# Recurrent states of a streaming encoder: two at a time inside the last feed-forward

## The chip, the cores and the metric

The kernel runs on one core of a Trainium2 chip. The metric is device time in microseconds (us), read as the median of several runs. A core has five engines with a queue of their own each: TensorE (PE in the profile, its weight loads PEld), VectorE (DVE), ScalarE (ACT), GpSimd (POOL), and SyncE (SP), which here only issues DMAs. An engine takes its instructions in the order in which they stand in its queue.

## The reference

Two layers of an encoder work on 512 frames of a new stream and on 8 running streams of 16 frames each, 640 rows of 1024 channels. Each layer is a feed-forward, a mixer, and another feed-forward, each followed by a LayerNorm of `ALPHA * x + sublayer(x)`. The feed-forward is

```
def swiglu(x, w_gate, w_up, w_down):
    return (jax.nn.silu(x @ w_gate) * (x @ w_up)) @ w_down
```

with 2816 hidden channels. The mixer of the second layer carries a recurrent state of 32 heads x 64 x 128 for each running stream, and the new state is an output:

```
h_new = h * jnp.exp(cs[:, -1])[..., None, None] + jnp.einsum('bsgr,bsgn,bsgrp->bgrpn', to_end, b_c, x_c)
```

It is a scaling of the old state by one number for each head, plus a product over the 16 new frames. All is in fp32.

## The kernel before

The kernel does six phases in turn: `ffn0`, `mix0`, `ffn1`, `ffn2`, `mix1`, `ffn3`. Every fp32 operand of a product is split into a high part (a cast on ScalarE, L100) and the rest (a subtraction on VectorE, L101), and three products of the parts stand for one. Weights come as tiles of 128 x 1024 through four `raw` places (L119, L340, L341, L468 issue the loads, all on SP).

**The feed-forward** (`ffn`, L226) takes 22 tiles of 128 hidden channels. Two go ahead; then five groups of four follow. In a group, `pair` (L399) does two tiles at a time: the gate products, and the up products, with a scheme of seven products of blocks for eight (`matrix`, L369, 84 matmuls at L365 for one call). Between the gate and the up products of a group's first pair stands the down projection of the group before (`down`, L535). In `ffn1`, `ffn2` and `ffn3` a down projection of four tiles is `down7` (L462), again seven products (L501), each for two row tiles, ahead of which the row tile of the running streams is done with 24 plain matmuls (L146). The seven products share six PSUM banks. Of each product, one row tile is added to `yacc` by VectorE (L510). The other is scaled by ScalarE into one of three `ev` buffers (L513), and a DMA that accumulates, issued by GpSimd, adds it to `yacc` (L514). The first and the second of these accumulations go to the same part of `yacc`. The first and the last down projections of a feed-forward are done with plain matmuls.

**The states.** The new states of the running streams are not made in the mixer. It leaves the rows that are needed in memory (`xb`), and the decays (`el`). `ssd_states` (L1457) makes the states inside `ffn3`: it is a generator, and `tick` (L235) advances it by one step at certain places: behind each gate and each up product pair, behind some row tiles of the first and the last down projection, and in `down7` behind its second and its fifth product (L530). That makes seven calls in the first group of four tiles (gate, three in the down projection, up, gate, up), six in each of the other four (gate, two in the down projection, up, gate, up), and three in the last down projection.

There are 32 states (4 groups of heads x 8 streams) of 128 x 512. For two streams at a time, twelve row loads (L1473 into `xrow`, L1474 into `brow`) bring three copies of 16 rows for each. Then, for each of the two: a load of the old state (L1478) into one of two places `h0`; and in the next step the product (L1481, one matmul into a bank of `pst`), the scaling by the decay on GpSimd (L1483), the addition of the product on VectorE (L1484), and the store (L1485). All loads and stores are issued by SP. In the profile `h0` is written `h`, and `pst` is written `bank`.

A scheduler lays out each engine's queue ahead of time. It goes by the order in which the instructions are written and by when it expects their inputs: an instruction whose inputs are ready can be placed ahead of one that was written before it. A tile with several places makes a new user wait until the last reader of the place is done.

Of the kernel before, what the change touches and what calls it, by code (L numbers as in the profile page):

```python
# [9 lines left out]
F32 = mybir.dt.float32  # L10
# [3 lines left out]
ALU = mybir.AluOpType  # L14
# [22 lines left out]
def kernel(ctx: ExitStack, tc: tile.TileContext, I, O, phases=PHASES):  # L37
    nc = tc.nc
# [1418 lines left out]
    def ssd_states(wk):  # L1457

        el8 = wk.tile([128, 4, 8, 8], F32, name="el8")
        nc.sync.dma_start(el8.rearrange("p g b h -> p g (b h)"), ssd["el"])  # L1460


        xrow = wk.tile([128, 512], F32R, name="xrow", bufs=1)
        brow = wk.tile([128, 2, 128], F32R, name="brow", bufs=1)
        nc.vector.memset(xrow.bitcast(F32), 0.0)
        nc.vector.memset(brow.bitcast(F32), 0.0)
        for g, b2, q in ((g, b2, q) for g in range(4) for b2 in range(2) for q in range(2)):
            for h in range(2):
                for r, (sx, sb) in enumerate(((0, 0), (0, 1), (1, 0))):
                    rows = slice(64 * h + 16 * r, 64 * h + 16 * r + 16)  # L1470
                    t0 = 64 * h + 32 * b2 + 16 * q
                    src = lambda s, a, b: ssd["xb"][g][s, t0:t0 + 16, a:b]
                    nc.sync.dma_start(xrow[rows].bitcast(F32), src(sx, 0, 512))  # L1473
                    nc.sync.dma_start(brow[rows, h].bitcast(F32), src(sb, 512, 640))  # L1474
            for h in range(2):
                n = 4 * h + 2 * b2 + q
                h0 = wk.tile([128, 512], F32, name="h0", bufs=2)
                nc.sync.dma_start(h0, I["ssd_h0"][g, n])  # L1478
                yield
                pst = state["pst"]()  # L1480
                nc.tensor.matmul(pst, brow[:, h], xrow, start=True, stop=True)  # L1481
                h4 = h0.rearrange("p (h d) -> p h d", d=64)
                nc.gpsimd.tensor_tensor(h4, h4, el8[:, g, n, :, None].to_broadcast([128, 8, 64]), op=ALU.mult)  # L1483
                nc.vector.tensor_tensor(h0, h0, pst, op=ALU.add)  # L1484
                nc.sync.dma_start(O["ssd_s"][g, n], h0)  # L1485

    def mixer1(ph, last):
        V, G = nc.vector, nc.gpsimd
# [391 lines left out]
    for ph in phases:  # L1880
        last = ph == phases[-1]
        if ph.startswith("ffn"):
            ffn(int(ph[3]), ph, last, sides.get(ph))
        elif ph == "mix0":
            mixer0(ph, last)
        else:
            mixer1(ph, last)
            if "ffn3" not in phases:
                with ExitStack() as st:
                    for _ in ssd_states(pool("ssd", 1, st, reuse_waits="tile")):  # L1890
                        pass
# [112 lines left out]
```

## Time and profile before

| | us |
|---|---|
| median of 3 runs | 2552.12 |
| lowest, highest | 2546.31, 2556.58 |
| profiled execution | 2550.71 |
| its span, first to last instruction | 2549.0 |
| weight load by SP in the whole profile, `w_gate`, to landing | 3.6 |
| accumulating DMA in the whole profile, to landing | 5.3 |

The side work lies between 2109 us, where the first row load is issued, and 2531 us, where the last state is stored. In rows of the timeline the columns are start and duration in us, engine, line, operation, output and input tiles, shape and count, and in brackets the idle time of the engine just before, with the instruction or DMA that ended it. Rows of waits give the waiting engine with its line, what it waited for, the total in us, the number of times, and the longest. A group of instructions by line is followed by its busy us, the mean of one in ns, and the idle time before it.

### The profile page before, as it was taken

What the parts mean: (1) busy time and instruction counts of PE and PEld (TensorE: products, weight loads), DVE (VectorE), ACT (ScalarE), POOL (GpSimd) and SP (SyncE); (2) the same over time, 40 slices, a digit from 0 to 9 for tenths busy, and PEclk for the clock granted to TensorE, in tenths of its full rate; (3) what the DMA queues carried; (4) which work ended last, traced back from release to release, by engine and by line L of the source; (5) the groups of instructions that cost most, each with busy time, mean ns of one, the idle gap of its engine ahead of it and who ended that gap; (6) DMA issues with size and microseconds to landing.
All of it is one profiled execution on the core that took longest, in us unless ns stands there. A gap on an engine that the chain in (4) does not pass through costs nothing. (4 is left out here: it accounts for less than half of the span.)

```text
span 2549.0 us, 40847 instructions
## 1 busy us (share of the span) xinstructions
PE 2501.2 (98%) x15551; PEld 2289.7 (90%) x15551; DVE 2013.0 (79%) x3505; ACT 1273.8 (50%) x2389; POOL 374.5 (15%) x492
## 2 busy tenths in 40 slices
PE   9999999999999999999999999999999999999998
PEld 9999999878789999999999999988989889898887
DVE  7788777666879888878988887777576789898877
ACT  4443444436744555554555554566565543555542
POOL 0000001210130000013000002211121251111111
PEclk9999999999999999999999999999999999999999
DMA  5332335443222433361244443456464723445553
GB/s 185 108 106 87 105 112 154 147 165 110 73 83 63 117 102 108 105 170 50 67 120 112 112 119 103 136 182 196 142 212 140 242 66 107 146 146 155 162 161 123
DMA packets 179253, 324.80 MB, mean 127 GB/s; under 512 B 21312, under 2 KB 92608, under 8 KB 178544
## 3 DMA queue, kind: packets, MB, share of 16 engines
q1 hardware_dynamic: 165200, 293.83, 36.5%
q0 software_dynamic: 13856, 28.35, 5.8%
q8 instruction: 122, 2.00, 0.3%
q14 instruction: 75, 0.61, 0.1%
HBM read 259.56 MB, written 40.54 MB: 118 GB/s over the span
## 5 line engine op out<-in xcount | busy, mean ns | idle before, releaser
L101 DVE TENSOR_TENSOR w<-raw,w 128x512 fp32r<-128x512 f32 (+2 forms) x721 | 627.6, 892 | 94.9 <-ACT w L100 92.0
L100 ACT CAST w<-raw 128x512 fp32r<-128x512 f32 (+1 forms) x721 | 532.7, 769 | 324.7 <-DVE raw L348 153.0
L365 PE MATMUL bank<-xhi,w 128*128 128x320 f32 x2432 | 540.6, 309 | 2.1 <-DVE hf L417 1.3
L146 PE MATMUL bank<-xhi,w 128*128 128x256 f32 (+2 forms) x2272 | 498.1, 311 | 1.6 <-ACT xhi L210 1.0
L365 PE MATMUL bank<-T,w 128*128 128x320 f32 x2736 | 427.0, 309 | 2.8 <-ACT bank L382 2.3
L365 PEld LDWEIGHTS bank<-xhi,w 128*128 128x128 f32 x2432 | 407.4, 188 | 8.4 <-DVE hf L417 3.7
L365 PEld LDWEIGHTS bank<-T,w 128*128 128x128 f32 x2736 | 406.9, 188 | 4.2 <-ACT bank L382 2.8
L146 PEld LDWEIGHTS bank<-xhi,w 128*128 128x128 f32 x2272 | 377.7, 188 | 11.6 <-issue 5.2
L365 PE MATMUL bank<-xlo,w 128*128 128x320 f32 x1216 | 375.0, 308 | 0.0
L146 PE MATMUL bank<-xlo,w 128*128 128x256 f32 (+2 forms) x1136 | 351.2, 310 | 1.9 <-DVE xlo L211 1.7
L146 PE MATMUL bank<-w,h 128*128 128x512 f32 x1488 | 346.6, 391 | 0.0
L146 PEld LDWEIGHTS bank<-w,h 128*128 128x128 f32 x1488 | 277.4, 188 | 57.3 <-ACT h L100 1.4
L365 PEld LDWEIGHTS bank<-xlo,w 128*128 128x128 f32 x1216 | 228.0, 188 | 0.0
L146 PEld LDWEIGHTS bank<-xlo,w 128*128 128x128 f32 x1136 | 213.9, 188 | 4.9 <-DVE xlo L211 2.0
L348 DVE TENSOR_TENSOR raw<-raw 128x512 f32<-128x512 f32 x304 | 210.7, 693 | 3.2
L514 POOL DMA_DIRECT2D yacc<-ev x84 | 73.6, 943 | 693.7 <-ACT ev L513 600.2
L501 PE MATMUL bank<-w,h 128*128 128x512 f32 x576 | 139.2, 396 | 6.9 <-ACT ev L513 6.9
L501 PEld LDWEIGHTS bank<-w,h 128*128 128x128 f32 x576 | 109.8, 191 | 31.2 <-ACT ev L513 8.2
L378 ACT COPY mx<-bank 128x320 f32<-128x320 f32 x152 | 64.7, 426 | 110.1 <-PE bank L365 109.5
L510 DVE SCALAR_TENSOR_TENSOR yacc<-bank,yacc 128x512 f32<-128x512 f32 x84 | 57.8, 689 | 69.3 <-PE bank L501 69.2
L223 DVE SCALAR_TENSOR_TENSOR yacc<-bank,yacc 128x512 f32<-128x512 f32 x120 | 81.8, 686 | 34.4 <-PE bank L146 33.9
L513 ACT ACTIVATE ev<-bank 128x512 f32<-128x512 f32 x84 | 50.3, 599 | 115.4 <-PE bank L501 95.1
(431 smaller groups left out, 3440.4 us busy)
## 6 DMA issues: line engine op xcount, KB each, us to landing
raw<-in_w_gate_dram SPq DMA_DIRECT2D x88, 512.0 KB, 3.6
raw<-in_w_up_dram SPq DMA_DIRECT2D x88, 512.0 KB, 4.1
raw<-in_w_down_dram SPq DMA_DIRECT2D x88, 512.0 KB, 3.6
raw<-in_m_in_dram SPq DMA_DIRECT2D x52, 512.0 KB, 4.6
yacc<-ev POOLq DMA_DIRECT2D x84, 256.0 KB, 5.3
raw<-in_m_out_dram SPq DMA_DIRECT2D x24, 512.0 KB, 4.2
csb<-cs_d SPq DMA_DIRECT2D x20, 512.0 KB, 5.4
h<-in_ssd_h_dram SPq DMA_DIRECT2D x16, 512.0 KB, 6.2
```

What stands on the lines that cost most here:

```text
L100: nc.scalar.copy(hi, src)
L101: return nc.vector.tensor_tensor(lo, src, hi.bitcast(F32), op=ALU.subtract)
L146: state["pe"] = nc.tensor.matmul(ps, a, b, start=(k == 0), stop=(k == n - 1)).ins
L223: state["acc"] = nc.vector.scalar_tensor_tensor(ya, pb, scale, ya, op0=ALU.mult, op1=ALU.add).ins
L348: V.tensor_tensor(o, v, w, op=ALU.subtract)
L365: nc.tensor.matmul(ps, A[p][:, a, k * 128:k * 128 + 128], X[p][b][:, k, :], start=(first and n == 0), stop=(n == 11), skip_group_check=True)
L378: nc.scalar.copy(e[n], ps)
L501: nc.tensor.matmul(ps, a[:, u], b[:, v], start=(first and n == 0), stop=(n == 5), skip_group_check=True)
L510: V.scalar_tensor_tensor(ya, ps, 0.5 / ALPHA, ya, op0=ALU.mult, op1=ALU.add)
L513: nc.scalar.mul(e, ps, 0.5 / ALPHA)
L514: nc.gpsimd.dma_start(yacc[:, t, 512 * j:512 * j + 512], e, accum_op=ALU.add)
```

## The change

Both states of a pair are handled in one step of the generator, and moves and arithmetic are in different steps. One step issues the stores of the pair before, the twelve row loads and the two loads of old states. The next does, for each of the two, the scaling, the product and the addition. The last pair is stored behind the loop. `h0` has three places in place of two, so that 2 KB more are taken in each partition while `ffn3` runs. The scaling is now written ahead of the product. The number of steps stays at 32, with the end of the generator in the 33rd call.

```diff
+        done = []
         for g, b2, q in ((g, b2, q) for g in range(4) for b2 in range(2) for q in range(2)):
+            for o, h0 in done:
+                nc.sync.dma_start(o, h0)
             for h in range(2):
                 for r, (sx, sb) in enumerate(((0, 0), (0, 1), (1, 0))):
                     rows = slice(64 * h + 16 * r, 64 * h + 16 * r + 16)
...
                     nc.sync.dma_start(xrow[rows].bitcast(F32), src(sx, 0, 512))
                     nc.sync.dma_start(brow[rows, h].bitcast(F32), src(sb, 512, 640))
+            done = []
             for h in range(2):
                 n = 4 * h + 2 * b2 + q
-                h0 = wk.tile([128, 512], F32, name="h0", bufs=2)
-                nc.sync.dma_start(h0, I["ssd_h0"][g, n])
-                yield
+                done.append((O["ssd_s"][g, n], wk.tile([128, 512], F32, name="h0", bufs=3)))
+                nc.sync.dma_start(done[h][1], I["ssd_h0"][g, n])
+            yield
+            for h, (_, h0) in enumerate(done):
+                h4 = h0.rearrange("p (h d) -> p h d", d=64)
+                nc.gpsimd.tensor_tensor(h4, h4, el8[:, g, 4 * h + 2 * b2 + q, :, None].to_broadcast([128, 8, 64]),
+                                        op=ALU.mult)
                 pst = state["pst"]()
                 nc.tensor.matmul(pst, brow[:, h], xrow, start=True, stop=True)
-                h4 = h0.rearrange("p (h d) -> p h d", d=64)
-                nc.gpsimd.tensor_tensor(h4, h4, el8[:, g, n, :, None].to_broadcast([128, 8, 64]), op=ALU.mult)
                 nc.vector.tensor_tensor(h0, h0, pst, op=ALU.add)
-                nc.sync.dma_start(O["ssd_s"][g, n], h0)
+            yield
+        for o, h0 in done:
+            nc.sync.dma_start(o, h0)
```

## The prediction

> **What bounds the kernel now.** I read the page's busy shares first, then stretches of the timeline, then TensorE's waits, then the chain of waits around the longest of them.
>
> ```profile
> span 2549.0 us, 40847 instructions
> PE 2501.2 (98%) x15551; PEld 2289.7 (90%) x15551; DVE 2013.0 (79%) x3505; ACT 1273.8 (50%) x2389; POOL 374.5 (15%) x492
> ```
>
> The span is 2549.0 us and TensorE is busy for 2501.2 of it. The change touches only the last feed-forward, so I asked for the busy time of that stretch (up to TensorE's last product), and of 100 us of an earlier feed-forward with the same products and no side work. Columns: stretch, its length, busy us of PE, PEld, DVE, ACT, POOL, granted clock, DMA share, GB/s.
>
> ```profile
> 1420.00:1520.00 100.00, 100.00 (x575) 92.26 (x574) 80.11 (x119) 51.74 (x83) 9.49 (x11) 1.00 0.44 117
> ...
> 2107.00:2540.00 433.00, 422.45 (x2468) 391.21 (x2467) 371.72 (x578) 198.80 (x337) 71.89 (x67) 0.99 0.49 144
> ```
>
> TensorE idles 433.00 - 422.45 = 10.55 us here and none at all there. The change adds and removes no product, so these 10.55 us and whatever a lowered clock costs are all that it can win. TensorE's waits in the last feed-forward, longest first, are led by one group, and three rows of TensorE's timeline hold it:
>
> ```profile
> PE bank L501 <- ACT ev L513: 6.9, 3, 3.4
> ```
> ```profile
> 2311.65 4.61 PE L501 MATMUL bank<-w,h 128*128 128x512 f32 x12 [3.41 <-ACT ev L513]
> ...
> 2390.81 3.01 PE L501 MATMUL bank<-w,h 128*128 128x512 f32 x12 [1.72 <-ACT ev L513]
> ...
> 2468.52 4.59 PE L501 MATMUL bank<-w,h 128*128 128x512 f32 x12 [1.79 <-ACT ev L513]
> ```
>
> Each is the last product of one of the three later seven-product down projections (bracket: idle before it). They idle 3.41 + 1.72 + 1.79 = 6.92 us. The twelve matmuls behind them are slow too. The chain around the first shows what twelve cost undisturbed, and what they wait for:
>
> ```profile
> 2291.47 5.44 PE bank L501 x24
> ...
> 2303.26 0.48 POOL yacc L514
> ...
> 2303.78 7.12 DMA yacc<-ev
> ...
> 2311.00 0.61 ACT ev L513
> ...
> 2311.65 4.61 PE bank L501 x12
> ```
>
> 24 take 5.44, so 12 take 2.72; the three groups lose 1.89, 0.29 and 1.87, together 4.05 us. So the stall is worth 6.92 + 4.05 = 10.97 us. It waits for an eviction (L513), that for one of three `ev` buffers, and that for an accumulating DMA which GpSimd issues (L514). I followed GpSimd's queue back to the first accumulation of each projection, with the eviction that feeds it:
>
> ```profile
> 2292.86 0.60 ACT L513 ACTIVATE ev<-bank 128x512 f32<-128x512 f32 x1 [0.17 <-PE bank L501]
> ...
> 2373.71 0.60 ACT L513 ACTIVATE ev<-bank 128x512 f32<-128x512 f32 x1
> ...
> 2451.35 0.60 ACT L513 ACTIVATE ev<-bank 128x512 f32<-128x512 f32 x1 [0.17 <-PE bank L501]
> ```
> ```profile
> 2293.48 1.38 POOL L1483 TENSOR_TENSOR h<-h,el 128x512 f32<-128x512 f32 x1 [9.86 <-DMA h<-in_ssd_h_dram]
> 2294.80 0.89 POOL L514 DMA_DIRECT2D yacc<-ev  x1
> 2303.24 2.65 POOL L514 DMA_DIRECT2D yacc<-ev  x3 [7.55 <-ACT ev L513]
> ...
> 2375.71 0.89 POOL L514 DMA_DIRECT2D yacc<-ev  x1
> ...
> 2453.29 0.88 POOL L514 DMA_DIRECT2D yacc<-ev  x1
> ```
>
> The evictions end at 2293.46, 2374.31 and 2451.95; the accumulations go at 2294.80, 2375.71 and 2453.29, which is 1.34, 1.40 and 1.34 us later. The first row shows why: the scaling of a state (L1483) stands ahead of the accumulation in GpSimd's order and has waited for its load. The second accumulation adds to the same part of `yacc` as the first and so waits until that has landed; the third and fourth stand behind it. A late first one therefore shifts the whole chain. The load comes late because of SP's queue:
>
> ```profile
> 2286.90 0.41 SPq L1485 DMA_DIRECT2D out_ssd_s_dram<-h  x1
> 2287.36 0.43 SPq L1474 DMA_DIRECT2D brow<-xb_d  x1
> 2289.11 0.35 SPq L340 DMA_DIRECT2D raw<-in_w_up_dram  x1
> 2289.56 0.38 SPq L1478 DMA_DIRECT2D h<-in_ssd_h_dram  x1
> ```
>
> The store of the state before (needs VectorE's addition), then a weight load (needs a free `raw` place), and only then the load. The other half of the stall is how long accumulations take. From the DMA issues (count, KB, us to landing), first of the second feed-forward, then of the last:
>
> ```profile
> yacc<-ev POOLq DMA_DIRECT2D x21, 256.0 KB, 5.3
> ```
> ```profile
> h<-in_ssd_h_dram SPq DMA_DIRECT2D x32, 256.0 KB, 3.4
> out_ssd_s_dram<-h SPq DMA_DIRECT2D x32, 256.0 KB, 2.1
> yacc<-ev POOLq DMA_DIRECT2D x28, 256.0 KB, 6.3
> ```
>
> 5.3 us without the states' traffic, 6.3 with it.
>
> **The change part by part.** Work is conserved: 32 products, 32 scalings, 32 additions, 32 loads, 32 stores and 192 row loads before and after, in 33 steps. Counted over the calls of the side work (seven in the first group of four tiles, six in each later group), an even call now computes and an odd one stores and loads. So in each later group the call ahead of the down projection computes, the one behind its second product only moves data, and the one behind its fifth product computes.
>
> ```profile
> L1483 POOL TENSOR_TENSOR h<-h,el 128x512 f32<-128x512 f32 x32 | 42.9, 1342 | 275.3 <-DMA h<-in_ssd_h_dram 218.3 <-DVE raw L478 26.6 <-DVE s L407 20.0
> ...
> L1484 DVE TENSOR_TENSOR h<-h,bank 128x512 f32<-128x512 f32 x32 | 21.7, 680 | 4.8 <-PE bank L1481 4.4 <-issue 0.4
> ```
>
> *Scaling a step behind its load.* The states computed ahead of a down projection were loaded at least one step earlier, so their scalings are over before it, and the first accumulation can go as its eviction ends. That takes 1.34, 1.40 and 1.34 us out of the three stalls, which become 2.07, 0.32 and 0.45: gain 4.08 us. If GpSimd still holds the accumulation, the gain is nothing.
>
> *The lowered clock.* 1.79 us of idle cost 1.87 and 1.72 cost 0.29, so idle of 0.32 and 0.45 should cost nothing: gain up to 0.29 + 1.87 = 2.16. The first stall, at 2.07, lies above both, so I leave its 1.89. Rows of the granted clock after the second and third:
>
> ```profile
> 2391.00:2393.00 2.00, 2.00 (x10) 1.00 0.42 147
> ...
> 2470.00:2472.00 2.00, 2.00 (x6) 0.50 0.52 137
> ```
>
> The Trainium skill (TensorE: Matmul & The Clock Gate, Part 1: The HAM clock gate) says that the clock halves after an idle window of about 3.4 us. Here 1.79 us was enough for 0.50, so the measurement decides; by the page a stall of 2.07 us would keep the full clock and all 4.05 us would come back: 8.1 us ahead of the costs below, against 6.2.
>
> *SP's queue.* A step of moves is two stores, twelve row loads and two state loads, 16 issues. The pitch of such a run is 2276.09 - 2275.62 = 0.47 us:
>
> ```profile
> 2275.62 0.42 SPq L1474 DMA_DIRECT2D brow<-xb_d  x1
> 2276.09 0.42 SPq L1473 DMA_DIRECT2D xrow<-xb_d  x1
> ```
>
> That is 7.5 us in one run instead of two runs of about 2 and 14 issues. Weight loads behind it (L340, L341, L468) start up to 7.5 us later; today the second run already puts 6.6 us in front of some, and no weight load appears among TensorE's waits, so I cost it at nothing; if that cover were gone, the step's extra 0.9 us per pair would be paid, 14 us over 16 pairs. The store now waits for an addition of an earlier step, so it holds nobody. With three places, the second load waits for the first store of the pair before to land, 2.1 us, while the twelve row loads in between fill 5.6: hidden.
>
> *Additions in pairs.* A second addition waits 0.68 us for the first, and a VectorE instruction behind the pair waits 0.68 more than now. VectorE is busy for 372 of the 433 us, so I bound this between 0 and 0.68 x 3 = 2 us at the three projections and take 0.3.
>
> *Bytes beside the accumulations.* In each of those projections two pairs of stores and loads now come in bursts, at the call ahead of it and at the one behind its fifth product. The nearest rows are 5.3 and 6.3 us: at best the traffic leaves the accumulations alone (1 us for each of two in the chain, 6 us over three projections), at worst it costs as much again. The bytes are the same and I see no reason for either sign, but a burst is more likely to meet the first accumulation, so I take a loss of 0.3 us a projection, 0.9.
>
> Sum: 4.08 + 2.16 - 0.3 - 0.9 = 5.0 us. The profiled execution took 2550.7 us, 1.4 below the median of the three runs (2552.1), so I expect 2545.7 for such an execution and a median of **2547**.
>
> **The rivals.** *A, the forecast:* 2547.
>
> *B, the whole stall goes:* the first accumulation goes earlier and lands faster too. 10.97 us less than the median is 2541. For: no such stall where there is no side work. Against: it needs both halves at once.
>
> *C, nothing to measure:* the instructions do not keep to their steps. For: the `brow` load at 2287.36 belongs to the following call, and was issued as soon as the product had freed its rows; scalings, too, run as soon as their load lands. Then the second state of a pair is still loaded late, or the accumulations meet a thicker burst that eats the 5 us: 2552. The Trainium skill (DMA: Bandwidth & Descriptors, Issuing engines are not separate DMA queues) states a rule that speaks for this: transfers of all issuing engines run on the same 16 engines and interleave. The 6.3 against 5.3 us above agrees.
>
> *D, slower:* a pair's second scaling takes its place ahead of the first accumulation, as one does now, but its load stands behind two stores and twelve row loads. 14 x 0.47 = 6.6 us after the computing call, plus 3.4 to land and 1.34 to scale, is 11.3; today the accumulation goes 2294.80 - 2285.80 = 9.0 us after the call's product.
>
> ```profile
> 2285.80 0.23 PE bank L1481
> ```
>
> So the accumulation goes 2.3 us later, or 4.0 with a weight load's wait in front, as the one of 1.75 us between the issues at 2287.36 and 2289.11: I take 3.5 for each of three stalls, 2 for the first of the four projections, and the lowered clock in that one and in the second stall, 1.9 + 1.6: 10.5 + 2 + 3.5 = 16 us, 2568. It decides once that scaling precedes the accumulation and its load is issued later than 9.0 - 1.3 - 3.4 = 4.3 us after the product. Against: orders follow when a load is expected, and one behind 14 issues is expected late.
>
> **How the numbers follow.** A 0.45, B 0.15, C 0.25, D 0.15. Half a per cent, 12.8 us, is about what a measurement of this kernel can tell from no change. A, B and C all lie within it; B with a little luck beyond gives faster 0.05. D lies beyond it for most of its span: slower 0.12. Same 0.83. The range takes A, B but its end, C and the lower edge of D: 2539 to 2563.
>
> **What would show it.** Right: at the first accumulation of each down projection, GpSimd no longer comes out of a scaling, and it is issued within 0.2 us of its eviction; the three bracketed waits fall to about 2.1, 0.3 and 0.4; the stretch's idle falls from 10.55 to near 6. C shows as the same brackets with longer landings than 6.3; D as a scaling with a longer wait for its load right ahead of the first accumulation. Wrong altogether would be new waits for weights (L101, L365), or idle time of TensorE before L1481.

## The result and the profile after

| | before, us | changed, us |
|---|---|---|
| median of 7 runs each | 2549.5 | 2541.18 |
| lowest, highest | 2544.44, 2556.58 | 2537.88, 2543.43 |
| profiled execution | 2550.71 | 2543.04 |
| its span | 2549.0 | 2541.3 |

The changed kernel takes 0.9966 of the time before (95% interval 0.9952 to 0.998); the medians differ by 8.3 us. The forecast was a median of 2547; rival B, the whole stall gone, was 2541. The spans differ by 7.7 us. The page's head of the changed kernel:

```profile
span 2541.3 us, 40809 instructions
...
PE 2500.3 (98%) x15551; PEld 2289.3 (90%) x15551; DVE 2015.3 (79%) x3505; ACT 1272.5 (50%) x2389; POOL 376.2 (15%) x492
```

The same work is done; what went is time in which TensorE waited or ran slowly. Here is the last feed-forward up to TensorE's last product in busy time by stretches (us, then busy PE, PEld, DVE, ACT, POOL, granted clock, DMA share, GB/s), and below it TensorE's waits in it (total, times, longest).

```profile
2107.00:2533.00 426.00, 420.59 (x2472) 389.34 (x2470) 375.54 (x580) 197.74 (x337) 76.48 (x67) 1.00 0.50 146
```
```profile
PE bank L365 <- ACT bank L382: 1.6, 5, 0.4
PE bank L365 <- DVE s L407: 1.4, 3, 0.5
PE bank L365 <- DVE w L101: 0.7, 1, 0.7
PE bank L365 <- ACT mx L378: 0.7, 1, 0.7
PE bank L365 <- ACT w L100: 0.6, 1, 0.6
```

Idle time is 426.00 - 420.59 = 5.41 us, in place of 10.55. The wait of the products L501 for evictions, 6.9 us before, is not among the rows at all. But small waits of L365 have grown: these five rows give 5.0 us, where the kernel before has 2.6, in four rows:

```profile
PE bank L365 <- ACT bank L382: 1.0, 1, 1.0
PE bank L365 <- DVE hf L417: 0.9, 3, 0.4
PE bank L365 <- DVE w L101: 0.5, 1, 0.5
...
PE bank L365 <- DVE s L407: 0.2, 1, 0.2
```

The groups of TensorE's products in that stretch, by their shapes (busy us, mean ns, idle before), before and then changed:

```profile
L365 PE MATMUL bank<-T,w 128*128 128x320 f32 x684 | 107.4, 309 | 1.5 <-ACT bank L382 1.0 <-DVE w L101 0.5
...
L501 PE MATMUL bank<-w,h 128*128 128x512 f32 x192 | 49.5, 411 | 6.9 <-ACT ev L513 6.9
```
```profile
L365 PE MATMUL bank<-T,w 128*128 128x320 f32 x684 | 109.1, 310 | 3.0 <-ACT bank L382 1.6 <-DVE w L101 0.7 <-ACT w L100 0.6
...
L501 PE MATMUL bank<-w,h 128*128 128x512 f32 x192 | 44.8, 389 | 0.0
```

The same 192 matmuls take 49.5 - 44.8 = 4.7 us less. Most of that is the slow groups behind the stalls, which are gone with the stalls. Undisturbed, 24 such matmuls stand in one row:

```profile
2306.75 5.60 PE L501 MATMUL bank<-w,h 128*128 128x512 f32 x24
```

Twelve reach 2.72 us before the next one starts, so twelve take 5.60 - 2.72 = 2.88 us to the end of the last, and the rows of 4.61, 3.01 and 4.59 us before were 1.73, 0.13 and 1.71 too long, together 3.57. The stretch is 433 - 426 = 7.0 us shorter, of the 7.7 between the spans: 10.55 - 5.41 = 5.1 us are idle time, and 422.45 - 420.59 = 1.9 us are busy time. So half of what the slow matmuls gave was taken by other products: L365 has 1.7 us more. (Groups by line overlap at their ends, so their differences do not add up to the total.)

**The first accumulation.** ScalarE's eviction, GpSimd's queue, and SP's load of a state, around the second of the four seven-product down projections, then around the fourth, changed kernel:

```profile
2294.26 0.60 ACT L513 ACTIVATE ev<-bank 128x512 f32<-128x512 f32 x1 [2.88 <-PE bank L501]
...
2448.43 0.60 ACT L513 ACTIVATE ev<-bank 128x512 f32<-128x512 f32 x1 [2.88 <-PE bank L501]
```
```profile
2294.17 1.04 POOL L1486 TENSOR_TENSOR h<-h,el 128x512 f32<-128x512 f32 x1 [2.98 <-DVE yacc L522]
2295.15 0.88 POOL L514 DMA_DIRECT2D yacc<-ev  x1
2299.65 1.81 POOL L514 DMA_DIRECT2D yacc<-ev  x2 [3.61 <-DMA yacc<-ev]
...
2449.33 1.04 POOL L1486 TENSOR_TENSOR h<-h,el 128x512 f32<-128x512 f32 x1 [3.96 <-issue]
2450.31 0.87 POOL L514 DMA_DIRECT2D yacc<-ev  x1
```
```profile
2290.11 0.43 SPq L1482 DMA_DIRECT2D h<-in_ssd_h_dram  x1
```

A scaling (L1486, before L1483) still comes right ahead of the first accumulation, and it still waits for its load. The load goes at 2290.11, where it went at 2289.56 before, and lands 3.9 us later. The scaling starts 0.1 us after that, here and in the two later projections, whatever its bracket names. In the second projection the accumulation goes 2295.15 - 2294.86 = 0.29 us after the eviction's end, but in the fourth 2450.31 - 2449.03 = 1.28, nearly the 1.34 of before. What did change in every one is how long the accumulation then takes. The line of landing times of that one instruction, before and then changed:

```profile
DMA to landing us min/median/max: 7.7/7.7/7.7
```
```profile
DMA to landing us min/median/max: 3.8/3.8/3.8
```

For all 28 the median fell from 6.3 to 4.6 us.

SP's queue tells what the first accumulation met. Before, it was issued at 2294.80; the rows are SP's big loads near it:

```profile
2293.98 0.33 SPq L341 DMA_DIRECT2D raw<-in_w_up_dram  x1
2296.08 0.33 SPq L340 DMA_DIRECT2D raw<-in_w_gate_dram  x1
```

One 512 KB load went 0.8 us ahead and the next 1.3 us behind, with stores and rows from 2297 on. In the changed kernel it was issued at 2295.15:

```profile
2292.90 0.33 SPq L341 DMA_DIRECT2D raw<-in_w_up_dram  x1
2297.47 0.33 SPq L340 DMA_DIRECT2D raw<-in_w_gate_dram  x1
2298.60 0.33 SPq L341 DMA_DIRECT2D raw<-in_w_gate_dram  x1
2306.72 0.33 SPq L1477 DMA_DIRECT2D brow<-xb_d  x1
```

Here the nearest loads are 2.3 us away on either side, and no row or store of the states comes before 2306.72. The products of the pair (L1489) that the text of the change puts ahead of this down projection stand well before it:

```profile
2277.27 0.63 PE L1489 MATMUL bank<-xrow,brow 128*128 128x512 f32 x2
```

The scheduler drew them forward into the gate products, so the burst of stores, rows and loads behind them was out by 2290.5.

### The profile page after: what moved, and what is told of

Same layout as the page of the kernel before. It is cut to its first block, busy times and chain, and to the rows that moved or that the text cites. A ratio compares the mean times of both kernels' runs of the same rounds, so it can differ in the third digit from the quotient of the medians.

```text
span 2541.3 us, 40809 instructions
## 1 busy us (share of the span) xinstructions
PE 2500.3 (98%) x15551; PEld 2289.3 (90%) x15551; DVE 2015.3 (79%) x3505; ACT 1272.5 (50%) x2389; POOL 376.2 (15%) x492
## 5 line engine op out<-in xcount | busy, mean ns | idle before, releaser
L101 DVE TENSOR_TENSOR w<-raw,w 128x512 fp32r<-128x512 f32 (+2 forms) x721 | 625.0, 889 | 87.5 <-ACT w L100 84.7
L365 PE MATMUL bank<-xhi,w 128*128 128x320 f32 x2432 | 540.4, 309 | 2.9 <-DVE s L407 1.9
L365 PE MATMUL bank<-T,w 128*128 128x320 f32 x2736 | 428.7, 309 | 3.0 <-ACT bank L382 1.6
L365 PEld LDWEIGHTS bank<-xhi,w 128*128 128x128 f32 x2432 | 406.6, 188 | 8.8 <-DVE s L407 3.1
L365 PEld LDWEIGHTS bank<-T,w 128*128 128x128 f32 x2736 | 407.0, 188 | 6.3 <-ACT bank L382 4.2
L146 PEld LDWEIGHTS bank<-xhi,w 128*128 128x128 f32 x2272 | 380.0, 189 | 11.9 <-issue 5.1
L365 PE MATMUL bank<-xlo,w 128*128 128x320 f32 x1216 | 375.0, 308 | 0.0
L365 PEld LDWEIGHTS bank<-xlo,w 128*128 128x128 f32 x1216 | 228.0, 187 | 0.0
L501 PE MATMUL bank<-w,h 128*128 128x512 f32 x576 | 134.5, 389 | 0.0
L501 PEld LDWEIGHTS bank<-w,h 128*128 128x128 f32 x576 | 108.1, 188 | 22.5
```

The lines of the kernel that those rows point to most:

```text
L101: return nc.vector.tensor_tensor(lo, src, hi.bitcast(F32), op=ALU.subtract)
L146: state["pe"] = nc.tensor.matmul(ps, a, b, start=(k == 0), stop=(k == n - 1)).ins
L365: nc.tensor.matmul(ps, A[p][:, a, k * 128:k * 128 + 128], X[p][b][:, k, :], start=(first and n == 0), stop=(n == 11), skip_group_check=True)
L501: nc.tensor.matmul(ps, a[:, u], b[:, v], start=(first and n == 0), stop=(n == 5), skip_group_check=True)
```

## The experiments

All ratios are to the kernel before, run beside it, with 95% intervals. Two readings serve throughout: the *hold* of a first accumulation (its issue less the end of its eviction) and the *landings*. After the first runs they could be put into one sum. The products' evictions share three `ev` places, and the last product (fourth product of the scheme, into banks `x`) waits for the sixth accumulating eviction, which needs the place of the third accumulation. The third is issued right behind the second, and the second waits until the first has landed. So the chain is: hold + (first to third issue) + landing of the third, from the end of the first eviction. Each is read from the start and the landing of the single instructions. TensorE's own products set the deadline: undisturbed, the last product starts 14.6 us after the end of the first eviction (2309.47 - 2294.86 in the changed kernel), and the sixth eviction, 0.6 us, stands between the third landing and it, which leaves 14.0.

| kernel | chain in the four projections, us | TensorE's idle at L501 behind evictions, us |
|---|---|---|
| before | 10.8, 17.4, 15.7, 15.8 | 0, 3.41, 1.72, 1.79 |
| changed | 11.5, 11.2, 11.9, 11.1 | none |
| before, no scaling | 10.6, 11.9, 11.9, 11.6 | none |
| changed, one step later | 13.7, 14.1, 14.2, 13.3 | none |
| before, three places | 10.6, 11.5, 11.7, 11.8 | none |
| changed, two places | 15.7, 13.7, 14.9, 14.4 | 1.64, 0, 0.83, 0.34 |
| before, rows once | 13.2, 13.2, 12.6, 12.9 | none |
| changed, scaling on ScalarE | 12.0, 11.6, 11.6, 12.4 | none |
| changed, no scaling | 11.2, 11.1, 11.9, 11.6 | none |
| changed, held again | 12.5, 13.7, 13.4, 16.4 | 0, 0, 0, 2.37 |
| changed, twin stores | 12.4, 12.2, 13.7, 11.6 | none |
| changed, twin stores and hold | 12.6, 14.3, 13.7, 16.8 | 0, 0.27, 0, 2.41 |

All nine stalls have chains of 14.3 us or more. Eight equal the chain less 14.0; the ninth (16.8) equals the chain less 14.4, as TensorE itself came to its last product 0.3 us later there. The 39 chains of 14.2 or less show no such wait; the two above 14.0 among them, both of one step later, cost 0.2 us or less. The expectations of the last two experiments speak of 14.4 and of sums up to 0.4 us longer than these: they took the issues of a run to be 0.9 us apart, and some are only 0.5 apart.

**Without the scaling** (before)

```diff
-                h4 = h0.rearrange("p (h d) -> p h d", d=64)
-                nc.gpsimd.tensor_tensor(h4, h4, el8[:, g, n, :, None].to_broadcast([128, 8, 64]), op=ALU.mult)
```

> The kernel before without the scaling on GpSimd (L1483): the states come out unscaled, every load, store, product and addition stays. Theory H (the first accumulation is held in GpSimd's queue by a scaling that waits for its load): the accumulation goes within 0.2 us of its eviction, the three waits of TensorE on the evictions shrink from 3.4, 1.7 and 1.8 us to about 2.1, 0.3 and 0.4, the time falls by 4 to 6 us. Theory T (the accumulations land late because row loads, stores and state loads run beside them, 6.3 us against 5.3 without): landings stay over 6 us, the three waits stay within half a us, the time falls by 0 to 2 us.

2532.48 us, ratio 0.9939 (0.9926 to 0.9951). Holds are 0.3 us, the stall is gone, and the gain, 17.5 us by the medians, is larger than the stall's 11 us. Neither theory had that. First landings fell only to 5.6 to 5.7 in the later three (weight loads at 0.2 and 2.3 us behind the issue), and the third accumulations landed in 4.6 to 4.8 us in place of 6.4 to 7.1. So the scaling costs something besides the stall; the changed kernel without the scaling, below, shows that part alone.

**One step later** (changed)

```diff
+        yield
         done = []
```

> The changed kernel with one empty step ahead, so that the arithmetic stands behind the second product of a down projection and behind the up products, and the stores and row loads it frees come in the middle of the accumulations, as before the change; no scaling stands between accumulations in GpSimd's queue. H: as fast as the changed kernel, no waits on evictions, 7 to 9 us below before. T: landings of the accumulations back above 6 us, waits on evictions of 1 to 3 us in each of three down projections, 0 to 4 us below before.

2540.78 us, 0.9969 (0.9958 to 0.9981), as the changed kernel. First accumulations were held 0.3 us and landed in 3.3 to 4.0, but the states' traffic now fell into the middle of the projection and those from the third on took 5 to 10 us. The stalls of 1 to 3 us that traffic was to bring did not come: the chains were 13.3 to 14.2. The one wait on an eviction is of 0.4 us, ahead of a state's product. Long landings as such cost nothing while the chain stays under its deadline.

**The third place alone** (before)

```diff
-                h0 = wk.tile([128, 512], F32, name="h0", bufs=2)
+                h0 = wk.tile([128, 512], F32, name="h0", bufs=3)
```

> The kernel before with three places for a state in place of two, nothing else. H: the state whose scaling stands ahead of the first accumulation is loaded one state earlier, so nothing holds the accumulation: 4 to 6 us below before. T: the same bytes at nearly the same places beside the accumulations: waits of TensorE as before, within 2 us of before.

2540.12 us, 0.9965 (0.9951 to 0.9979): the whole gain, with the old order of steps. GpSimd's rows around the second projection:

```profile
2294.01 1.31 POOL L1483 TENSOR_TENSOR h<-h,el 128x512 f32<-128x512 f32 x1 [7.91 <-DMA h<-in_ssd_h_dram]
2295.27 0.89 POOL L514 DMA_DIRECT2D yacc<-ev  x1
2301.04 1.76 POOL L514 DMA_DIRECT2D yacc<-ev  x2 [4.88 <-DMA yacc<-ev]
```

The scaling still stands ahead, and still waits for its load. The hold is 0.71 us (the eviction ended at 2294.56) in place of 1.34, and the landing 5.1 us in place of 7.7. The second accumulation goes 5.77 us after the first, before 8.44. The third lands in 4.5 us in place of 7.1. So some 0.6 us less of hold came with some 2.6 us less of landing at either end of the chain. Neither pairs nor a step between move and scaling was needed.

**Pairs with two places** (changed)

```diff
-                done.append((O["ssd_s"][g, n], wk.tile([128, 512], F32, name="h0", bufs=3)))
+                done.append((O["ssd_s"][g, n], wk.tile([128, 512], F32, name="h0", bufs=2)))
```

> The changed kernel with two places for states in place of three: both loads of a pair wait for the stores of the pair before. The two scalings of a pair stand between the second and the third accumulation of a down projection, and the arithmetic of the call ahead of the projection is no longer drawn 9 us forward. H: the third accumulation and those behind it are held until the second load has landed: TensorE waits 3 us or more in each of four down projections, 5 to 20 us slower than before. T: the burst of stores, rows and loads meets the first and second accumulations, landings of 6 us or more, within 4 us of before.

2542.38 us, 0.9978 (0.9969 to 0.9987). It is not slower than before, as the view of the hold had it. Stalls are back, without a hold of the first accumulation; rows of GpSimd, of SP and of TensorE at the first projection:

```profile
2216.87 0.92 POOL L514 DMA_DIRECT2D yacc<-ev  x1 [20.16 <-ACT ev L513]
2225.84 0.87 POOL L514 DMA_DIRECT2D yacc<-ev  x1 [8.06 <-issue]
2226.41 2.37 POOL L1486 TENSOR_TENSOR h<-h,el 128x512 f32<-128x512 f32 x2
2228.41 2.12 POOL L514 DMA_DIRECT2D yacc<-ev  x2
```
```profile
2215.78 0.90 SPq L1482 DMA_DIRECT2D h<-in_ssd_h_dram  x2
2216.77 0.38 SPq L340 DMA_DIRECT2D raw<-in_w_up_dram  x1
2217.25 0.38 SPq L341 DMA_DIRECT2D raw<-in_w_up_dram  x1
```
```profile
2232.98 3.39 PE L501 MATMUL bank<-w,h 128*128 128x512 f32 x12 [1.64 <-ACT ev L513]
```

The accumulation goes 0.30 us after its eviction (2215.97 + 0.60), but among two state loads and two weight loads, 1.5 MB within 1.5 us, and lands in 8.4 us. Two scalings then stand between the second and the third accumulation, which goes 2.6 us after the second, where with nothing between them it goes 0.5 after it. The chain is 15.7 us and the stall 1.64. Without those two scalings the chain would be under 14, so the long landing alone would not have stalled TensorE here. In three of the four projections it is so; in the second, where no weight load was issued less than 1.5 us from it, the first landed in 3.8, and there is no stall.

**Rows loaded once** (before)

```diff
-                    nc.sync.dma_start(xrow[rows].bitcast(F32), src(sx, 0, 512))
-                    nc.sync.dma_start(brow[rows, h].bitcast(F32), src(sb, 512, 640))
+                    if (g, b2, q) == (0, 0, 0):
+                        nc.sync.dma_start(xrow[rows].bitcast(F32), src(sx, 0, 512))
+                        nc.sync.dma_start(brow[rows, h].bitcast(F32), src(sb, 512, 640))
```

> The kernel before with the twelve row loads only for the first pair, so that all states get the product of the first pair's rows; 180 of 192 row loads are left out. Theory R (the row loads slow the accumulations): the first accumulations of the later three down projections land in 4 us and the waits on evictions go. Theory C (a weight load of 512 KB issued from 1 us before to 2 us after an accumulation slows it): the landing goes by the nearest weight load alone: still 6 us or more where one is issued less than 1.5 us after, under 5 where the nearest is 2 us away or more.

2537.29 us, 0.996 (0.9947 to 0.9972). It tells less than it was meant to: with 180 row loads fewer the scheduler also put the scaling behind the first accumulation (hold 0.3 us), so both causes moved at once. The first accumulations landed in 4.3 to 5.9 us with hardly a row load left, each with a weight load issued less than 0.7 us from it.

**The scaling on ScalarE** (changed)

```diff
-                nc.gpsimd.tensor_tensor(h4, h4, el8[:, g, 4 * h + 2 * b2 + q, :, None].to_broadcast([128, 8, 64]),
-                                        op=ALU.mult)
+                for d in range(8):
+                    nc.scalar.mul(h4[:, d], h4[:, d], el8[:, g, 4 * h + 2 * b2 + q, d:d + 1])
```

> The changed kernel with the scaling on ScalarE, eight instructions of 128x64 for a state in place of one on GpSimd: 256 more ScalarE instructions of an estimated 0.22 us, 56 us, beside 199 of 433 us that it is busy. Theory V: VectorE is rid of GpSimd, 3 to 8 us faster than the changed kernel, less what ScalarE's casts and evictions wait for the eight in a row (1.8 us for a state). Theory Q: nothing to win, 0 to 10 us slower.

2540.41 us, 0.9969 (0.9958 to 0.998): no gain over the changed kernel. The group of eight scalings a state and TensorE's longest wait:

```profile
L1487 ACT ACTIVATE h<-h,el 128x64 f32<-128x64 f32 x256 | 64.2, 339 | 3.5 <-DVE hf L417 3.0 <-DMA h<-in_ssd_h_dram 0.4
```
```profile
PE bank L365 <- ACT bank L382: 5.4, 5, 1.4
```

What GpSimd no longer took from VectorE (next experiment) ScalarE took from its own evictions: 64.2 us in 256 pieces, and 5.4 us of TensorE's waits for them.

**The changed kernel without the scaling**

```diff
-                h4 = h0.rearrange("p (h d) -> p h d", d=64)
-                nc.gpsimd.tensor_tensor(h4, h4, el8[:, g, 4 * h + 2 * b2 + q, :, None].to_broadcast([128, 8, 64]),
-                                        op=ALU.mult)
```

> The changed kernel without the scaling on GpSimd (states come out unscaled). Without it the kernel before became 15.5 us faster, 7 more than by the whole change, while its VectorE splits (L101) took 6.9 us less. Theory V (GpSimd's scaling also slows VectorE's two-input instructions beside it): VectorE's busy time in the last feed-forward falls by 8 to 12 us, TensorE's small waits there go, 5 to 9 us faster than the changed kernel. Theory Q (the gain was only from GpSimd's queue): nothing is left to hold, within 2 us of the changed kernel.

2533.36 us, 0.9943 (0.9926 to 0.9959): about 8 us less than the changed kernel, whose chains have no stall to give. Two rows of the changed kernel and then the same two without the scaling: the busy time of one stretch, and VectorE's subtractions of the weight split in it (count, shortest, median and longest in ns):

```profile
2107.00:2520.00 413.00, 407.75 (x2417) 379.02 (x2416) 362.74 (x562) 197.74 (x337) 73.03 (x65) 1.00 0.51 148
```
```profile
L101 DVE TENSOR_TENSOR w<-raw,w x144: 676/1210/1941, 2107.1 to 2501.0; 128x512 fp32r<-128x512 f32 x74, 128x1024 fp32r<-128x1024 f32 x70
```
```profile
2107.00:2520.00 413.00, 412.76 (x2450) 385.71 (x2449) 358.88 (x573) 197.49 (x337) 29.85 (x33) 1.00 0.51 150
```
```profile
L101 DVE TENSOR_TENSOR w<-raw,w x143: 682/693/1230, 2112.6 to 2491.8; 128x512 fp32r<-128x512 f32 x73, 128x1024 fp32r<-128x1024 f32 x70
```

With the scaling on GpSimd, TensorE idles 5.25 us of the 413 and a subtraction can take 1.94 us; without it, 0.24 and 1.23. VectorE's busy time in the whole kernel falls by 11.0 us, from 2015.3 to 2004.3; 8 to 12 were expected for the last feed-forward. The Trainium skill (SBUF — State Buffer, Who interferes with whom) says that a VectorE operation on two tensors in SBUF contends with GpSimd's reads of SBUF; L101 subtracts two SBUF tiles, and the trace agrees. That the 8 us come by way of VectorE is read from these rows and not shown by itself: moving the scaling to ScalarE freed VectorE too, but cost as much elsewhere. This part of the cost is in both kernels, and the change did not touch it.

**Held again** (changed)

```diff
+                state.setdefault("held", None)
...
+                    if ph == "ffn3" and (a, j) == (0, 0) and state["held"] != fs[0]:
+                        state["held"] = fs[0]
+                        nc.gpsimd.tensor_scalar_mul(e, e, 1.0)
                     nc.gpsimd.dma_start(yacc[:, t, 512 * j:512 * j + 512], e, accum_op=ALU.add)
```

> The changed kernel with one more GpSimd instruction in each of the four seven-product down projections: a multiplication of the first evicted tile by 1.0, in place, between its eviction and its accumulation, which holds the accumulation for about 1 us as the scaling did before the change. Theory C: held, the accumulation goes 1 to 1.5 us ahead of the next weight load in place of 2 or more, and lands in 5 to 7.5 us in place of 3.3 to 3.8; waits on evictions of 1 to 3 us come back in the later three, 3 to 9 us slower than the changed kernel. Theory H (only the hold itself counts): landings stay under 4.5 us, the chain has about 2 us to spare, no waits, within 2 us of the changed kernel.

2543.31 us, 0.9981 (0.9971 to 0.9991), about 2 us over the changed kernel, which by the intervals is not certain. The holds are 1.9, 2.4, 2.5 and 4.3 us, more than ever before, and yet only the fourth stalls:

```profile
2465.56 3.06 PE L502 MATMUL bank<-w,h 128*128 128x512 f32 x12 [2.37 <-ACT ev L514]
```

Its chain is 16.4; in the others the first lands in 5.2 to 5.7 and the third in 4.3, and the chains stay at 12.5 to 13.7. A hold of 2.5 us alone is not enough for a stall.

**Twin stores, and twin stores with the hold** (changed). The stores of the first kernel; the second has the multiplication by one ahead of them as well, in the first two lines.

```diff
+                    if ph == "ffn3" and (state.get("nth", -1) + 1) % 7 == 0:
+                        nc.gpsimd.tensor_scalar_mul(e, e, 1.0)
                     nc.gpsimd.dma_start(yacc[:, t, 512 * j:512 * j + 512], e, accum_op=ALU.add)
+                    if ph == "ffn3":
+                        k = state["nth"] = state.get("nth", -1) + 1
+                        if k % 7 in (0, 2):
+                            nc.scalar.dma_start(dram.tile([128, 512], F32, name=f"twin{k}"), e)
```

> The changed kernel, and ScalarE also issues a store of the same 256 KB to spare memory right behind its eviction, for the first and the third accumulating eviction of each of the four seven-product down projections of the last feed-forward (eight stores). No hold is added. The theory to be tested is a sum: hold of the first accumulation, plus the time from its issue to that of the third, plus the third's landing, counted from the end of the first eviction; TensorE stalls by what the sum exceeds 14.4 us (17.8, 16.0 and 16.2 before gave 3.4, 1.7 and 1.8 us; the sums of the changed kernel are 11.0 to 11.9). That traffic at the time of issue makes the landing long: the first lands in 5 to 7 us in place of 3.3 to 3.9, the third in 5.5 to 7.5, the sums become 13 to 15, the stalls are 0 to 0.6 us each, and the time stays within 2 us of the changed kernel's 2541. That the landing goes by the hold or by GpSimd's work and not by traffic: the first still lands in 3.3 to 4.2 us and the sums stay below 12.5.

> The same with a multiplication by one on GpSimd of the first evicted tile ahead of its accumulation in each of the four, which alone (on the changed kernel) gave holds of 1.9 to 4.3 us, sums of 13 to 16.7, one wait of 2.4 us and 2543. By the sum and traffic: sums of 15 to 18, a stall of sum less 14.4 in most of the four, 3 to 9 us in all, 2544 to 2549. If traffic adds nothing to the hold: as the multiplication alone, one wait of about 2.4 us, 2543. If the stall does not follow the sum, waits on evictions appear where the sum is below 14 or are absent where it is above 15.

2539.32 us, 0.9965 (0.9951 to 0.9978), and 2544.0, 0.9986 (0.9975 to 0.9997). The stores themselves were issued on ScalarE's queue. A 256 KB store beside it made the first accumulation land in 5.1, 4.8, 4.7 and 3.6 us, against 3.9, 3.8, 3.3 and 3.6 in the changed kernel: up to 1.3 us more, so that only the first came to the 5 to 7 us expected. So traffic counts, but 256 KB outward is not what two 512 KB loads are. The chains were expected at 15 to 18 us with the hold and were 12.6 to 16.8; the stalls followed them, not the expectation:

```profile
2304.68 3.10 PE L501 MATMUL bank<-w,h 128*128 128x512 f32 x12 [0.27 <-ACT ev L513]
...
2461.73 3.21 PE L501 MATMUL bank<-w,h 128*128 128x512 f32 x12 [2.41 <-ACT ev L513]
```

They are at chains of 14.3 and 16.8 us, 14.0 and 14.4 above the idle; none at 12.6 and 13.7. The first half of that theory, the sum, held; the second, its size of the traffic, did not.

## Why the prediction was right and wrong

**The bound** was named rightly: the three stalls behind `ev`. All 6.92 us of idle went, and with them the slow matmuls. They were worth 3.57 us and not 4.05: the forecast took 2.72 us for twelve undisturbed matmuls, which leaves out the end of the last one, and 2.88 is what their rows have.

**The scaling a step behind its load** was put at 4.08 us, because "their scalings are over before it". This step failed. The scaling still comes right ahead of the first accumulation and out of its load, and the holds fell by 1.05, 0.73 and 0.06 us, together 1.84. The products of a pair were drawn forward, the loads behind them followed, and so the scaling of the next pair stands where that of the next state stood. The reason was the wrong one too: the step between load and scaling was not needed, as the third place alone gives the same time.

**Bytes beside the accumulations** were put at a loss of 0.9 us ("I see no reason for either sign"). This is the term that decided. First landings fell from 7.7, 6.7 and 6.3 us to 3.8, 3.3 and 3.6, together 10.0 us. The third accumulations, which end the chain, landed in 5.5, 6.0 and 5.1 us in place of 7.1, 6.4 and 7.1, another 4.1. Each chain was 1.7 to 3.4 us over its deadline, so the holds alone would have left stalls in all three, and the first landings alone would have removed all three. The bytes are the same, but their places are not: the median landing of 6.3 against 5.3 was taken for a general price of the traffic, where the trace held the price of each accumulation, and the loads beside it. That 7.7 us in the one with the longest stall stood among loads at -0.8 and +1.3 us was to be read in the rows of before.

**The lowered clock** was put at 2.16, since a stall of 2.07 us was left; none was left, so all of it came back. The length of an idle time does not tell its price. Before, the granted clock fell to 0.50 behind 1.79 us of idle, and twelve matmuls took 1.71 us longer; behind 1.72 us it stayed at 1.00, and they took 0.13 longer. Behind 2.37 us in the kernel held again, and behind 2.41 us with twin stores and hold, it stayed at 1.00 as well, here the row of the first:

```profile
2466.00:2469.00 3.00, 3.00 (x16) 2.44 (x15) 2.54 (x5) 1.68 (x3) 2.02 (x3) 1.00 0.67 190
```

Those twelve took 3.06 and 3.21 us, 0.18 and 0.33 over 2.88. The Trainium skill (TensorE: Matmul & The Clock Gate, Part 1: The HAM clock gate) speaks of a free-running window of activity of about 3.4 us. A price that goes by where the idle falls in a window would fit these rows; none of them shows the window itself.

**Additions in pairs** were put at 0.3, with 2 at most. New small waits of L365 took 2.4 us and L365 itself 1.7. They are not shown to come from the pairs: the third place alone in the old order has waits of much the same size, shown below. In the changed kernel four of them, 2.1 us of the 5.0, run back along ScalarE's and VectorE's queues to a VectorE instruction that a scaling stretched, such as a subtraction of 128x384 that took 1.40 us in place of 0.55 (2275.43, beside the scaling at 2275.17); the one of 0.56 us has two additions in a row behind it as well.

```profile
PE bank L365 <- DVE hf L417: 2.3, 4, 0.7
PE bank L501 <- DVE yacc L510: 1.1, 1, 1.1
PE bank L365 <- ACT bank L382: 0.8, 1, 0.8
```

**SP's queue** at nothing: right. No wait for a weight load's landing stands among TensorE's waits; the waits for weight splits (1.3 us, before 0.5) run back to VectorE.

**The sum.** It came to 5.0 us, mostly out of a term that did not come, and the fall was 8.3 by the medians. That 2541 still lies in the range is owed to the range, which was drawn to hold most of rival B; B is nearer to what happened than the forecast was.

**The rivals.** B happened. It had 0.15 because it "needs both halves at once". In the kernel with three places both halves did move at once: 0.6 us less hold and 2.6 us less landing. Two conditions that move together are not two independent chances. What the kernel held again shows against it is that a hold of 1.9 to 2.5 us brings the landings back only in part, to 5.2 to 5.7 us; pairs with two places show the long landing without the hold. So neither always brings the other; as far as the rows go, what counts is which loads are issued beside the accumulation, and the hold moves it among them. D's order did come: the scaling of a pair's second state stands ahead of the first accumulation, and its load goes 12.8 us after the products (2290.11 - 2277.27), far later than D's 4.3. But the products had been drawn some 9 us forward, where D counted from a product at its written place, and so the load went only 0.55 us later than before, and the accumulation 0.3 us behind its eviction. C's doubt, that instructions do not keep to their steps, was well founded, and it worked in the kernel's favour.

**Left open:** how much each neighbour adds to a landing. The landings go with the loads issued beside them (below), but the runs do not give the price of each: one store beside the accumulation added up to 1.3 us, and nothing tried gives 7.7 us from one neighbour. VectorE's work at the same time was not varied. Two rows, the 3 us from the issue of a first accumulation that landed in 7.7 us before, and of one that landed in 3.3 us in the changed kernel, show that neither a busy VectorE (3.00 and 2.93 us) nor the bytes then moved (221 and 206 GB/s) tell them apart:

```profile
2294.80:2297.80 3.00, 3.00 (x15) 2.49 (x14) 3.00 (x5) 1.40 (x2) 0.89 (x2) 1.00 0.87 221
```
```profile
2372.30:2375.30 3.00, 3.00 (x15) 2.49 (x14) 2.93 (x4) 2.03 (x3) 0.87 (x2) 1.00 0.90 206
```

## What to carry to other kernels

Follow a stall back through the buffers to a sum of terms with a deadline, here 14.0 us, and ask how far each variant lies from it: a chain that is over it by 3 us and one under it by 3 differ by all of the stall, and what is under it gains nothing more. Read the landing time of each DMA on that chain with what was issued within 2 us of it, instead of the median of its kind. Before a reordering in several parts, try its smallest part: one more buffer gave here what two at a time, a step ahead and a new order gave together.

## What the runs showed that was not expected

- The same 256 KB accumulating DMA lands in 3.3 to 8.4 us. Of the 36 first accumulations in the nine kernels without twin stores or an added hold, 15 have no weight load and no state load issued less than 1.0 us from them, and land in 3.3 to 4.2 us; the other 21 have at least one, and land in 4.3 to 8.4 but for one, with state loads alone, in 3.8. The three of the kernel before (6.3 to 7.7) have a second weight load 1.2 to 1.3 us behind; with three places it comes 1.9 us behind, and they land in 5.0 to 5.1.
- GpSimd's 32 scalings (44.5 us busy, off the critical path) cost the changed kernel 8 us: the longest weight subtraction on VectorE is 1.94 us with them and 1.23 without.
- A multiplication by one on GpSimd of 128x512 in place took 1.50 us in three of the four projections of the kernel held again and 2.46 in the fourth. Why is not shown.
- TensorE's granted clock fell to 0.50 behind 1.79 us of idle and stayed at 1.00 behind 2.37 and 2.41 us.
